# Layer 0's SwiGLU channel mixer in seven half-size products, beside plain context columns, with the layer norms around it in stages

## The chip, the core and the metric

The kernel runs on one core of one Trainium2 chip. A core has five engines, each with its own in-order queue: TensorE (PE; PEld is its weight load), VectorE (DVE), ScalarE (ACT), GpSimd (POOL) and SyncE (SP), which here only issues DMAs. TensorE writes into 8 PSUM banks of 128 x 512 floats; everything else works from SBUF. The metric is the device time in microseconds of one execution, median over runs. The profile is of one such execution.

## What is computed

A trunk of two layers over 1024 latent tokens and 256 context tokens, width 1024. Layer 0 has a recurrent and gated mixer, layer 1 attention; each layer ends with a SwiGLU channel mixer of hidden width 2816. Context tokens need layer 0 whole, and of layer 1 only keys and values. In layer 0, for the latent tokens (the context has the same with its own gates):

```python
def swiglu(h, w_in, w_out):
    gate, up = jnp.split(h @ w_in, 2, axis=-1)
    return (jax.nn.silu(gate) * up) @ w_out
...
        h = layer_norm(alpha * h + g1 * y, ln1_g[l], ln1_b[l])
        h = layer_norm(alpha * h + g2 * swiglu(modulate(h, sh2, sc2), ffn_w_in[l], ffn_w_out[l]),
                       ln2_g[l], ln2_b[l])
```

## The kernel before

All products are of float32 numbers split in two: a rounded high part (`rnd`: on ACT L69, on DVE L71) and the rest (`rest`, L77, on DVE), both float32r, and each product is three matmuls, `mm3` (L80 high by high, L81 high by low, L82 low by high). Tokens stand in ten blocks of 128: 0 to 3 and 4 to 7 are latent, 8 and 9 are the context.

Layer 0 after its mixer runs so. `layer0_out` does the out-projection (tiles `op`) for blocks 0 to 3, then for 4 to 9; ACT copies the banks out (L897), POOL multiplies by the gate (L699). `ln_steps` is the layer norm, a list of small steps that other loops call one by one (`pump`): on DVE the residual (L726), the statistics (L729) and the normalising (L743), on PE eight transposes for each block (`lnT`, L755), on ACT the modulation (L760) and the rounding into the operand tiles `ah`, on DVE the rests `al`, on POOL the affine part (L781, L782). `ffn` is the channel mixer. It runs twice, for blocks 0 to 3 (512 columns) and for 4 to 9 (512 and 256 columns). For each of 22 hidden tiles of 128 it loads three weight tiles (`fraw`), splits them (`fwh`, `fwl`), makes gate and up (`fi`: 8 slices of the contraction, 3 matmuls each, for either), applies SiLU (L1000) and the product (L1003); for two hidden tiles together it then multiplies into the output (`fo`), whose banks DVE adds to the sums in SBUF (L1035). The layer norm of blocks 4 to 9 runs inside the first of these calls; the second layer norm of blocks 0 to 3 inside the second; that of blocks 4 to 9 inside layer 1's input projection (`layer1_in`, tiles `l`), which does the units of blocks 0 to 3 first.

Layer 1's channel mixer, which the change doesn't touch, is already done by a recursion in the manner of Strassen, for its 1024 latent tokens: the tokens, the contraction and the gate and up columns are each cut in half, and seven products of sums and differences take the place of eight (`fi_jobs`, `fo_jobs`; the stationary tiles are `sop` and `fop`, sums of token halves are `T`). The hidden numbers go through HBM (`sd_d`) between the halves. Its code and its trace (2402 us to the end) stand beside layer 0's.

Of the kernel before, what the change touches and what calls it, by code (L numbers as in the profile page):

```python
# [37 lines left out]
def kernel(  # L38
# [64 lines left out]
    sd_d = dram.tile([NHT // 2, 7, 128, 512], F32, name="sd_d")  # L103
    qt_d = dram.tile([16, 128, LAT], F32, name="qt_d")
# [584 lines left out]

    def gate_rows(l, piece, ws):  # L690
        g = {}
        for w in ws:
            g[w] = lnp.tile([128, D], F32, tag=f"g{w}", name=nm("gate"))
            a = ada_d[2 * l + w:2 * l + w + 1, piece * D:(piece + 1) * D]
            nc.sync.dma_start(out=g[w], in_=a.broadcast_to([128, D]))
        return g

    def gate_mul(a, bb, hs, g):
        nc.gpsimd.tensor_tensor(out=a[:, hs], in0=a[:, hs], in1=g[int(bb >= 8)][:, hs], op=ALU.mult)  # L699

    def ln_steps(l, g, b, blocks, acc, mod, aT, src=None, dst=None, alpha=False, late=False, stats=None):

        C = {}

        def consts():
            C["g"] = lnp.tile([128, D], F32, tag="lng", name=nm("lng"))
            nc.sync.dma_start(out=C["g"], in_=g[l:l + 1, :].broadcast_to([128, D]))  # L710
            C["b"] = lnp.tile([128, D], F32, tag="lnb", name=nm("lnb"))
            nc.sync.dma_start(out=C["b"], in_=b[l:l + 1, :].broadcast_to([128, D]))

        def load(bb):
            h = lnp.tile([128, D], F32, tag="hin", name=nm("hin"))
            nc.sync.dma_start(out=h, in_=h_rows(src, bb))
            C["h", bb] = h

        def s0(bb):
            if src is not None:  # L720
                load(bb)

# [41 lines left out]
        def s5(bb):  # L764
# [5 lines left out]
            if not late:  # L770
                s55(bb)
# [19 lines left out]
        if now:  # L791
            consts()
# [1676 lines left out]
```

## Time and profile before

| | us |
|---|---|
| median of 3 runs | 3067.03 |
| lowest, highest | 3063.13, 3068.0 |
| the profiled execution's own time | 3063.5 |
| its span in the trace | 3061.6 |
| layer 0's channel mixer in the trace (first `fi` to last `fo`) | 694.7 to 1656.4 |

Mean granted clock of TensorE over the span: 0.982 of full speed. Times in the rows count from the span's start. A busy PE means that some matmul was under way; matmuls overlap, so the spacing of their starts, not their duration, is what each costs.

### The profile page before, as it was taken

What the parts mean: (1) busy time and instruction counts of PE and PEld (TensorE: products, weight loads), DVE (VectorE), ACT (ScalarE), POOL (GpSimd) and SP (SyncE); (2) the same over time, 40 slices, a digit from 0 to 9 for tenths busy, and PEclk for the clock granted to TensorE, in tenths of its full rate; (3) what the DMA queues carried; (4) which work ended last, traced back from release to release, by engine and by line L of the source; (5) the groups of instructions that cost most, each with busy time, mean ns of one, the idle gap of its engine ahead of it and who ended that gap; (6) DMA issues with size and microseconds to landing.
All of it is one profiled execution on the core that took longest, in us unless ns stands there. A gap on an engine that the chain in (4) does not pass through costs nothing. (4 is left out here: it accounts for less than half of the span.)

```text
span 3061.6 us, 37592 instructions
## 1 busy us (share of the span) xinstructions
PE 2897.3 (95%) x14341; PEld 2340.7 (76%) x14341; DVE 2100.9 (69%) x2742; ACT 1135.8 (37%) x2027; POOL 779.0 (25%) x757
## 2 busy tenths in 40 slices
PE   7999999987999999999999888898889899999997
PEld 4777777876888878888888777666767688888886
DVE  4898843658555566444446876999994777787778
ACT  2555522443211122111112535777773522222433
POOL 5323223246000022000003463777770000000002
PEclk9999999999999999999999999999999999999999
DMA  6344446753333332222223335021102243454854
GB/s 222 126 139 147 158 139 201 229 166 115 119 109 89 105 102 90 62 63 62 70 83 98 103 124 137 18 54 42 34 25 97 90 118 112 153 181 148 298 174 120
DMA packets 314931, 361.37 MB, mean 118 GB/s; under 512 B 16592, under 2 KB 230440, under 8 KB 309632
## 3 DMA queue, kind: packets, MB, share of 16 engines
q1 hardware_dynamic: 306496, 346.33, 35.9%
q0 software_dynamic: 2880, 5.31, 0.9%
q10 hardware_dynamic: 5376, 7.34, 0.7%
q8 instruction: 113, 1.85, 0.2%
q14 instruction: 66, 0.54, 0.1%
HBM read 295.14 MB, written 63.78 MB: 117 GB/s over the span
## 5 line engine op out<-in xcount | busy, mean ns | idle before, releaser
L80 PE MATMUL fi<-ah,fwh 128*128 128x512 f32 (+1 forms) x1056 | 382.4, 362 | 10.3 <-DVE fwh L71 10.3
L82 PE MATMUL fi<-ah,fwl 128*128 128x512 f32 (+1 forms) x1056 | 382.1, 362 | 6.4 <-DVE fwl L77 6.4
L81 PE MATMUL fi<-al,fwh 128*128 128x512 f32 (+1 forms) x1056 | 381.0, 361 | 0.0
L77 DVE TENSOR_TENSOR fwl<-fraw,fwh 128x1024 fp32r<-128x1024 f32 x132 | 168.6, 1277 | 204.4 <-ACT fwh L69 199.5
L699 POOL TENSOR_TENSOR acc<-acc,gate 128x512 f32<-128x512 f32 x40 | 61.1, 1561 | 876.3 <-DVE acc L1035 780.3
L80 PEld LDWEIGHTS fi<-ah,fwh 128*128 128x128 f32 x1056 | 201.2, 191 | 44.8 <-issue 7.8
L82 PEld LDWEIGHTS fi<-ah,fwl 128*128 128x128 f32 x1056 | 201.0, 190 | 42.0 <-DVE fwl L77 9.3
L81 PEld LDWEIGHTS fi<-al,fwh 128*128 128x128 f32 x1056 | 201.3, 191 | 33.1
L1000 ACT ACTIVATE sil<-fi 128x512 f32<-128x512 f32 x66 | 34.7, 526 | 504.7 <-PE fi L82 502.5
L1035 DVE TENSOR_TENSOR acc<-acc,fo 128x512 f32<-128x512 f32 x200 | 134.1, 685 | 81.5 <-PE fo L82 81.5
L73 POOL TENSOR_SCALAR th<-tf 128x512 fp32r<-128x512 f32 x236 | 165.1, 710 | 97.9 <-ACT tf L1761 93.9
L77 DVE TENSOR_TENSOR tl<-tf,th 128x512 fp32r<-128x512 f32 x204 | 171.2, 853 | 13.4 <-POOL th L73 12.4
L80 PE MATMUL ip<-ah,whi 128*128 128x512 f32 (+1 forms) x480 | 175.2, 365 | 3.6 <-ACT ah L69 3.5
L80 PE MATMUL fo<-fwh,hh 128*128 128x512 f32 x440 | 171.8, 390 | 0.1
L81 PE MATMUL ip<-al,whi 128*128 128x512 f32 (+1 forms) x480 | 171.4, 357 | 0.4 <-DVE al L77 0.4
L82 PE MATMUL fo<-fwh,hl 128*128 128x512 f32 x440 | 171.5, 390 | 0.0
L81 PE MATMUL fo<-fwl,hh 128*128 128x512 f32 x440 | 171.2, 389 | 0.0
L82 PE MATMUL ip<-ah,wlo 128*128 128x512 f32 (+1 forms) x480 | 170.4, 355 | 0.0
L1761 ACT COPY tf<-T 128x512 f32<-128x512 f32 x236 | 133.3, 591 | 41.7 <-PE T L1756 24.8
L80 PE MATMUL fi<-ah,sop 128*128 128x512 f32 x352 | 138.3, 393 | 4.8 <-ACT sop L69 4.8
L2291 POOL DMA_DIRECT2D acc<-h_d x16 | 14.2, 905 | 502.8 <-DMA wt<-sd_d 453.8
L1756 PE MATMUL T<-ident,P 128*128 128x128 f32 x944 | 140.5, 275 | 1.1 <-ACT tf L1761 0.4
(388 smaller groups left out, 7738.2 us busy)
## 6 DMA issues: line engine op xcount, KB each, us to landing
fraw<-in_ffn_w_in_dram SPq DMA_DIRECT2D x88, 512.0 KB
adaraw<-in_ada_w_dram SPq DMA_DIRECT2D x40, 1024.0 KB
fraw<-in_ffn_w_out_dram SPq DMA_DIRECT2D x44, 512.0 KB
sraw<-in_ffn_w_in_dram SPq DMA_DIRECT2D x44, 512.0 KB
wt<-sd_d SPq DMA_DIRECT2D x77, 256.0 KB
wt<-in_ffn_w_out_dram SPq DMA_DIRECT2D x55, 256.0 KB
h_d<-acc SPq DMA_DIRECT2D x26, 512.0 KB
sd_d<-hp SPq DMA_DIRECT2D x22, 512.0 KB
```

The source lines that it names most:

```text
L73: nc.gpsimd.tensor_scalar(out=o, in0=i, scalar1=1.0, scalar2=0.0, op0=ALU.mult, op1=ALU.add)
L77: e.tensor_tensor(out=o, in0=i, in1=hi.bitcast(F32), op=ALU.subtract)
L80: nc.tensor.matmul(ps, lhsT=sh, rhs=mh, start=start, stop=False)
L81: nc.tensor.matmul(ps, lhsT=sh, rhs=ml, start=False, stop=False)
L82: nc.tensor.matmul(ps, lhsT=sl, rhs=mh, start=False, stop=stop_)
L699: nc.gpsimd.tensor_tensor(out=a[:, hs], in0=a[:, hs], in1=g[int(bb >= 8)][:, hs], op=ALU.mult)
L1000: nc.scalar.activation(out=sil[si][:, :n], in_=ps_[:, :n], func=AF.Silu)
L1035: nc.vector.tensor_tensor(out=acc[bb][:, ns], in0=acc[bb][:, ns], in1=ps_, op=ALU.add)
L1756: nc.tensor.transpose(ps_[:, x_ * 128:(x_ + 1) * 128], st["P", i, h][:, j * 128:(j + 1) * 128], ident)
L1761: nc.scalar.copy(out=tf, in_=st.pop(("T", i, j)))
L2291: nc.gpsimd.dma_start(out=acc[bb][:, hs], in_=h_rows(3, bb)[:, hs], accum_op=ALU.add)
```

## The change

Layer 0 gets the seven products too. For the 1024 latent tokens the input half takes seven products of 4 slices of the contraction for each hidden tile in place of two times eight slices on both token halves; the 256 context columns are multiplied as before, by the four quarters A11, A12, A21, A22 of the weights (`context`). The hidden numbers, 512 latent and 128 context columns wide, go out to HBM (`sd0_d`) and come back in 77 steps of the output half, each of 15 matmuls into five banks, with a 512-wide weight tile and a 640-wide operand tile loaded and split for each step; here the context is folded into the seven products, one block in each half. The gate products now take the PSUM bank on DVE, the residual is added by an accumulating DMA that POOL issues (`add_rows`), the normalising moves from DVE to ACT, and the affine part moves from POOL to DVE. The layer norms run in stages: `tick` moves each block one stage on, twice in each job. `layer1_in` starts with blocks 4 to 7. In the diff, lines of code that only allocate are left out.

```diff
+    def add_rows(acc, stage, bb, h_):
+        hs = half_cols(h_)
+        nc.gpsimd.dma_start(out=acc[:, hs], in_=h_rows(stage, bb)[:, hs], accum_op=ALU.add)
...
+        groups = [TOK1, CTXB + TOK2]
+        LASTK = 3
+        seq = [(gi, nh, k) for gi in range(2) for nh in range(2) for k in range(12)][2:]
...
+        def u4a(bb):
+            o = blk_tg(bb)[1]
+            c = slice(o, o + 128)
+            (yh, yl), (b11, b11l) = aT[1], (t.bitcast(F32)[:, 0:4, c] for t in aT[0])
+            a, b = C["a", bb, 0], C["a", bb, 1]
+            t1, t2 = (ln0.tile([128, 4, 128], F32, tag=t, name=nm(t)) for t in ("t1", "t2"))
+            C["t", bb] = t1, t2
+            sub(t1, a, b11)
+            sub(t1, t1, b11l)
+            rnd("a", yh[:, 0:4, c], t1)
+            rnd("a", yh[:, 4:8, c], b)
+            sub(t2, b, t1)
+            rnd("a", T["T2"][0][:, :, c], t2)
+            sub(a, b, a)
+            rnd("a", T["T3"][0][:, :, c], a)
...
+        wait = [lambda bb: None] * 3
+        plain = wait + [s1, s2, s3, lambda bb: high_of(aT, C, bb), lambda bb: low_of(aT, C, bb)]
+        other = wait + [s1, s2, s3, u4a, u4b]
+        came = [0]
+        def tick():
+            one = False
+            for x in sorted(active, key=lambda x: (x[1] > 3, x[2])):
+                st_ = other if 4 <= x[0] < 8 else plain
+                if st_[x[1]] is s3:
+                    if one:
+                        continue
+                    one = True
+                st_[x[1]](x[0])
+                x[1] += 1
+                if x[1] == len(st_):
+                    active.remove(x)
...
+            mul(acc[bb][:, hs], ps_, gates[int(bb >= 8)][:, hs])
+            add_rows(acc[bb], 0, bb, nh)
+            if nh:
+                came[0] += 1
+                active.append([bb, 0, came[0]])
...
+            if gi and nh and k >= 12 - LASTK:
+                if k == 11:
+                    aT[1], aT[2] = new_aT(1), new_aT(2)
+                    for j, bb in enumerate(blocks):
+                        for i_ in range(i - LASTK + 1, i + 1):
+                            step_mm(j, i_)
+                        evac(bb, nh, bks[j], gates)
+                        tick()
...
+        def make_t4(bb):
+            c = slice(blk_tg(bb)[1], blk_tg(bb)[1] + 128)
+            t = P["fi"].tile([128, 4, 128], F32, tag=("old", "s4")[bb % 2], name=nm("t4"))
+            b21h, b21l = (x.bitcast(F32)[:, 4:8, c] for x in aT[0])
+            t2h, t2l = (x.bitcast(F32)[:, :, c] for x in T["T2"])
+            sub(t, b21h, t2h)
+            add(t, t, b21l)
+            sub(t, t, t2l)
+            split(B["T4"][0][:, :, c], B["T4"][1][:, :, c], t)
...
+        def done(what, j):
+            a, b = tA[j], tB[j]
+            if what == 2:
+                if j == 0:
+                    gates_in()
+                at(2, fn(gated, b, 0))
+                at(7, fn(statistics, FO["p"], acc2[b], C2, b, 0))
+            if what == 3:
+                at(1, fn(gated, b, 1))
+                for d, f in ((3, f1), (4, f2), (5, f3), (6, f4), (7, f5)):
+                    at(d + 2 * j, fn(f, b))
+            if what == 0:
+                at(1, fn(gated, a, 0))
+                at(5, fn(statistics, FO["p"], acc2[a], C2, a, 0))
+            if what == 1:
+                if j == 0:
+                    for k in sorted(plan):
+                        for f in plan.pop(k):
+                            f()
+                gated(a, 1)
...
+        def second(h):
+            for i, n in enumerate(("A21", "A22")):
+                t = P["zh"].tile([128, 2, 512], F32R, tag=("zA", "zB")[i], name=nm("sop"))
+                split(t[:, 0, :], t[:, 1, :], raws[h, 1][:, i * 512:i * 512 + 512])
+                opnd[h, n] = (t[:, 0, :], t[:, 1, :])
+            g, u = raws[h, 0], raws[h, 1]
+            sub(u[:, :512], g[:, :512], u[:, :512])
+            sub(u[:, 512:], u[:, 512:], u[:, :512])
+            add(g[:, :512], u[:, 512:], g[:, :512])
+            sub(g[:, 512:], g[:, 512:], u[:, 512:])
...
+        FACT = {1: ("A11", "B11"), 2: ("A12", "B21"), 5: ("S1", "T1"), 3: ("S4", "B22"), 6: ("S2", "T2"), 7: ("S3", "T3"),
+                4: ("A22", "T4")}
+        def context(h):
+            ps_ = bank("fi")
+            bh, bl = B["ctx"]
+            for i, n in enumerate(("A11", "A12", "A21", "A22")):
+                hi, lo = opnd[h, n]
+                if i == 2:
+                    tick()
+                for k in range(4):
+                    c = slice(k * 128, (k + 1) * 128)
+                    kk = 4 * (i % 2) + k
+                    mm3(ps_[:, 256 * (i // 2):256 * (i // 2) + 256], hi[:, c], lo[:, c], bh[:, kk, :], bl[:, kk, :],
+                        kk == 0, kk == KD - 1)
+            yield
+            hp = P["zh"].tile([128, 2, 640], F32, tag="hp", name=nm("hp"))
+            tmp["hp", h] = hp
+            v = lambda t: t.rearrange("p (a n) -> p a n", a=2)
+            nc.scalar.activation(out=hp[:, :, 512:640], in_=v(ps_[:, 0:256]), func=AF.Silu)
+            mul(hp[:, :, 512:640], hp[:, :, 512:640], v(ps_[:, 256:512]))
...
+        REST = ("c", 5, 3, 6, 7, 4)
+        seq = [(h, p) for h in range(E) for p in (1, 2)]
+        for h in range(NHT):
+            seq += [(h, p) for p in (REST if h < E else (1, 2) + REST)]
+        where = {x: j for j, x in enumerate(seq)}
+        ahead = [[] for _ in seq]
+        def put(at_, f):
+            ahead[at_].append((0, f))
+        for h in range(NHT):
+            a0 = where[h, 1]
+            if h >= E:
+                put(a0 - 9, fn(raw, h, 0))
+                put(a0 - 9, fn(raw, h, 1))
+            put(max(a0 - (3 if h >= E else 2), 0), fn(pair, h, 1 if h else 0, ("A11", "A12"), 0))
+            z = where[h - 1, 4] + 1 if h else 2
+            put(z, fn(second, h))
+            put(z, fn(pair, h, 2, ("S1", "S4"), 0))
+            put(where[h, 6] - (3 if h else 2), fn(pair, h, 0, ("S3", "S2"), 1))
+            if h >= NP:
+                put(where[h, 6], fn(old, h))
...
+        order = [0, 1, 5, 3, 4, 2, 6]
+        prods = (1, 7, 6, 4, 5, 2, 3)
+        wsrc = {1: (0, 0), 7: (1, 1), 6: (0, 0), 4: (1, 0), 5: (1, 1), 2: (1, 0), 3: (1, 1)}
+        LAST = 4
+        NS = 7 * NP
...
+        def load(s_):
+            x, i = divmod(s_, NP)
+            t = X[s_] = slot(s_)
+            load_w(t[:, 0:512], i, *wsrc[prods[x]])
+            nc.sync.dma_start(out=t[:, 512:1152], in_=sd0_d[i, order[x]])
...
+                for j in range(5):
+                    if x and i == 0 and j >= 2:
+                        evac(x - 1, j - 2)
+                    mms(s_, j)
+                if x and i == 1:
+                    evac(x - 1, 3)
+                    evac(x - 1, 4)
+                tick(s_)
...
+            ahead.append((6, fn(load, s_)))
+            if prods[s_ // NP] in (7, 6, 4, 5):
+                ahead.append((4, fn(comb, s_)))
+            ahead += [(3, fn(high, s_)), (2, fn(low, s_))]
...
-    in_units = [("k", 0), ("cq", 0), ("dq", 0), ("dq", 1), ("k", 2), ("k", 1), ("cq", 1), ("v", 2), ("v", 0), ("v", 1)]
+    in_units = [("k", 1), ("cq", 1), ("dq", 1), ("dq", 0), ("k", 2), ("k", 0), ("cq", 0), ("v", 2), ("v", 1), ("v", 0)]
...
-        aT0 = layer0_out(bks)
-        pairs = [[2 * i, 2 * i + 1] for i in range(NHT // 2)]
...
-        ffn(0, [(h, [(0, 0, 512)]) for h in pairs], aT0, accA, before=load_gates, ended=to_gate(accA))
...
-        ffn(0, [(h, [(1, 0, 512), (2, 0, 256)]) for h in pairs], aT0, accB, before=load_first, ended=ended)
...
+        aT1, acc, ready, pieces, fo, tq, affine_consts, K, close_fo = layer0_rest(bks)
```

On ACT, where the out-projection ends and the channel mixer starts, before: `acc` are the sums of the out-projection, `sil` and `hh` the hidden numbers of the first tile, `a` and `ah` the layer norm of blocks 4 to 9.

```order
L897 COPY acc_756_4970<-op_5019 128x512
L1000 ACT_TABLE_LOAD
L1000 ACTIVATE sil_5445<-fi_5420 128x512
L69 CAST hh_5493<-sil_5445 128x512
L1000 ACTIVATE sil_5539<-fi_5514 128x512
L69 CAST hh_5585<-sil_5539 128x512
L760 ACTIVATE a_877_5594<-lnT_5589,modc 128x128 x4
L69 CAST ah_827_5388<-a_877_5594 128x4x128
L760 ACTIVATE a_879_5605<-lnT_5600,modc 128x128 x4
L69 CAST ah_827_5388<-a_879_5605 128x4x128
```

After, at the same place, from the second block's normalising (L720) on: `sop` are the weights' first splits, `p` the first product's copy, `a`, `ah` and `acc` the layer norm of blocks 8, 9, 4 and on.

```order
L720 ACTIVATE acc_763_5018<-acc_763_5018,nb_5443,rs_5399 128x1024
L69 CAST sop_5474<-sraw_5466 128x1024
L69 CAST sop_5477<-sraw_5470 128x1024
L69 CAST ah_837_5333<-a_847_5427 128x4x128
L69 CAST ah_837_5333<-a_849_5437 128x4x128
L734 ACTIVATE a_866_5500<-lnT_5495,modc 128x128 x4
L734 ACTIVATE a_868_5510<-lnT_5505,modc 128x128 x4
L720 ACTIVATE acc_764_5021<-acc_764_5021,nb_5516,rs_5419 128x1024
L1511 COPY p_870_5525<-fi_5480 128x512
L69 CAST ah_837_5333<-a_866_5500 128x4x128
L69 CAST ah_837_5333<-a_868_5510 128x4x128
L734 ACTIVATE a_874_5542<-lnT_5537,modc 128x128 x4
```

Before, the layer norm of blocks 4 to 9 stood among the hidden tiles' work and nothing in the first `ffn` call read its result. After, its 6 blocks stand in one run, and the weights' splits and the copies of the first products stand among them.

On DVE, within one hidden tile (of blocks 4 to 9 before): `fraw` are loaded weights, `sil` the gate, `hl` the low part of the hidden numbers.

```order
L77 TENSOR_TENSOR fwl_9991<-fraw_9766,fwh_9990 128x1024
L77 TENSOR_TENSOR fwl_10051<-fraw_9826,fwh_10050 128x1024
L71 CAST fwh_10056<-fraw_9892 128x1024
L77 TENSOR_TENSOR fwl_10057<-fraw_9892,fwh_10056 128x1024
L1003 TENSOR_TENSOR sil_10021<-sil_10021,fi_10062 128x512
L77 TENSOR_TENSOR hl_10089<-sil_10021,hh_10088 128x512
L1003 TENSOR_TENSOR sil_10048<-sil_10048,fi_10092 128x256
L77 TENSOR_TENSOR hl_10119<-sil_10048,hh_10118 128x256
```

After, from the last product of one hidden tile into the next: `hp` are the tile's hidden numbers, `sraw` the loaded weights, `sop` their splits, `old` and `s` what is stored for the output half.

```order
L1128 TENSOR_TENSOR hp_7897<-p_1141_7827,fi_7981 128x512
L1131 TENSOR_TENSOR hp_7897<-hp_7897,sil_7842 128x512
L77 TENSOR_TENSOR sop_7997<-sraw_7781,sop_7997 128x512
L77 TENSOR_TENSOR sop_8000<-sraw_7781,sop_8000 128x512
L1125 TENSOR_TENSOR sraw_7781<-sraw_7779,sraw_7781 128x512
L1125 TENSOR_TENSOR sraw_7781<-sraw_7781 128x512
L1128 TENSOR_TENSOR sraw_7779<-sraw_7781,sraw_7779 128x512
L1125 TENSOR_TENSOR sraw_7779<-sraw_7779,sraw_7781 128x512
L77 TENSOR_TENSOR sop_8007<-sraw_7779,sop_8007 128x1024
L1125 TENSOR_TENSOR old_7938<-hp_7897,old_7938 128x640
L1128 TENSOR_TENSOR old_7938<-old_7938 128x640
L1125 TENSOR_TENSOR s_1165_8025<-hp_7897,old_7938 128x640
```

The sums and differences of weight halves and of hidden numbers are new on DVE, ahead of the split that the next products need.

## Rows read from the trace of the kernel before

**Rows 1.** The page, part 1: busy time, share of the span, instructions.
```profile
PE 2897.3 (95%) x14341; PEld 2340.7 (76%) x14341; DVE 2100.9 (69%) x2742; ACT 1135.8 (37%) x2027; POOL 779.0 (25%) x757
```

**Rows 2.** Windows of 50 us in steady channel-mixer stages, layer 0 first.
```profile
core 0: us, PE busy (x) PEld busy (x) DVE busy (x) ACT busy (x) POOL busy (x), PEclk, DMA share, GB/s
800.00:850.00 50.00, 50.00 (x217) 40.52 (x216) 25.78 (x32) 7.08 (x10) 0.00 (x0) 1.00 0.36 105
...
2500.00:2550.00 50.00, 50.00 (x222) 41.42 (x221) 39.48 (x53) 13.61 (x18) 4.21 (x2) 1.00 0.36 108
```

**Rows 3.** Groups by line and shape, TensorE: count, busy us, mean ns, idle before.
```profile
L80 PE MATMUL fi<-ah,fwh 128*128 128x512 f32 x704 | 283.7, 403 | 10.3 <-DVE fwh L71 10.3
L80 PE MATMUL fo<-fwh,hh 128*128 128x512 f32 x440 | 171.8, 390 | 0.1
```

**Rows 4.** Timeline of TensorE in layer 0: start, duration, engine, line.
```profile
814.50 0.39 PE L80 MATMUL fo<-fwh,hh 128*128 128x512 f32 x1
...
817.90 0.39 PE L80 MATMUL fo<-fwh,hh 128*128 128x512 f32 x1
...
1381.22 0.40 PE L80 MATMUL fi<-ah,fwh 128*128 128x512 f32 x1
...
1386.84 0.28 PE L80 MATMUL fi<-ah,fwh 128*128 128x256 f32 x1
...
1389.66 0.39 PE L80 MATMUL fo<-fwh,hh 128*128 128x512 f32 x1
```

**Rows 5.** Timeline of TensorE in layer 1's input half.
```profile
2600.18 0.39 PE L80 MATMUL fi<-ah,sop 128*128 128x512 f32 x1
...
2603.58 0.39 PE L80 MATMUL fi<-ah,sop 128*128 128x512 f32 x1
```

**Rows 6.** Windows of 50 us at the start of layer 0's channel mixer.
```profile
650.00:700.00 50.00, 41.64 (x164) 32.68 (x163) 24.54 (x24) 19.59 (x33) 15.51 (x9) 0.90 0.53 172
700.00:750.00 50.00, 44.73 (x192) 35.13 (x190) 43.06 (x48) 19.37 (x43) 25.79 (x16) 0.93 0.43 127
750.00:800.00 50.00, 41.91 (x174) 32.98 (x175) 36.97 (x38) 15.82 (x35) 18.64 (x9) 0.90 0.40 127
```

**Rows 7.** Timeline of ScalarE: one block of layer 1's layer norm, then splits.
```profile
2392.97 0.62 ACT L69 CAST ah<-a 128x512 fp32r<-128x512 f32 x1
2393.49 0.61 ACT L69 CAST T<-t 128x512 fp32r<-128x512 f32 x1
...
2394.53 1.24 ACT L2024 ACTIVATE acc<-acc,nb,rs 128x1024 f32<-128x1024 f32 x1
2396.69 2.90 ACT L2041 ACTIVATE a<-lnT,modc 128x128 f32<-128x128 f32 x8 [0.92 <-PE lnT L2033]
...
2403.02 1.04 ACT L69 CAST sop<-sraw 128x1024 fp32r<-128x1024 f32 x1 [0.76 <-DMA sraw<-in_ffn_w_in_dram]
...
2416.59 1.28 ACT L1146 ACT_TABLE_LOAD   x1
```

**Rows 8.** Issues of DMA: operation, count, size, median us to landing.
```profile
acc<-h_d POOLq DMA_DIRECT2D x16, 256.0 KB, 4.7
```

**Rows 9.** Window at the start of layer 1's input half.
```profile
2400.00:2450.00 50.00, 43.02 (x174) 34.18 (x175) 39.17 (x57) 24.90 (x39) 0.00 (x0) 0.90 0.29 80
```

**Rows 10.** Groups by line and shape, VectorE.
```profile
L77 DVE TENSOR_TENSOR sop<-sraw,sop 128x1024 fp32r<-128x1024 f32 x66 | 80.6, 1221 | 15.8 <-ACT sop L69 15.8
...
L77 DVE TENSOR_TENSOR sop<-sraw,sop 128x512 fp32r<-128x512 f32 x22 | 15.9, 723 | 2.6 <-ACT sop L69 2.6
...
L1072 DVE TENSOR_TENSOR sil<-p,fi 128x512 f32<-128x512 f32 x22 | 15.1, 687 | 26.6 <-PE fi L82 26.5
```

**Rows 11.** Window at the start of layer 1's output half.
```profile
2850.00:2900.00 50.00, 50.00 (x222) 41.44 (x221) 39.35 (x45) 25.03 (x26) 0.00 (x0) 1.00 0.83 293
```

**Rows 12.** Windows: second layer norm of blocks 0 to 3; layer 1's input projection.
```profile
1050.00:1200.00 150.00, 144.44 (x718) 120.36 (x717) 97.69 (x108) 36.13 (x75) 40.60 (x24) 0.98 0.32 102
1656.40:1880.00 223.60, 195.43 (x1126) 170.29 (x1124) 156.06 (x203) 97.18 (x195) 109.61 (x85) 0.93 0.46 138
```

More of the change, by code (lines that the diff above doesn't have):

```diff
@@ new lines, in layer0_rest @@
+                        evac(bb, nh, bks[j], gates)
+                tick()
+            if (nh == 1) and k < 2 * len(blocks) and k % 2 == 1 and k // 2 < len(blocks):
+                statistics(ln0, acc[blocks[k // 2]], C, blocks[k // 2], 0)
+            if i in (2, 6, 10):
+                fins.append(mod_cols(*mods.pop(0)))
+            if i in (6, 10, 14):
+                fins.pop(0)()
+        closed("s3", "accA")
+        P["tp"] = opened("tp", "right")
+        for n in ("T2", "T3"):
+            T[n] = [P["tp"].tile([128, 4, 512], F32R, tag=n + x, name=nm(n)) for x in "hl"]
@@ new lines, in layer0_rest, with open_fo, gates_in @@
+        jobs, flush = fi0_jobs(0, B, P, left, lambda: None if "fi" in P else tick(), make_t4, aside)
+        n = (half_cols(0), half_cols(1))
+        tA, tB = [0, 1, 2, 3, 8], [4, 5, 6, 7, 9]
+        FO, K = {}, {}
+        def open_fo():
+            flush()
+            flush()
+            closed("fi", "raw", "stash", "ring")
+            FO["p"] = opened("acc0")
+        def gates_in():
+            K["gate"] = [FO["p"].tile([128, D], F32, tag=f"g{w}", name=nm("gate")) for w in range(2)]
+            gate_rows(K["gate"], 0, 5)
@@ new lines, in layer0_rest, with at, tick2, gated @@
+        late_jobs, acc2, pieces = fo0_jobs(0, P, FO, open_fo, lambda *a: done(*a), lambda s_: tick2(s_), tA, tB)
+        C2, aT1 = {}, {}
+        plan, now = {}, [0]
+        def at(d, *fs):
+            plan.setdefault(now[0] + d, []).extend(fs)
+        def tick2(step):
+            now[0] = step
+            for f in plan.pop(step, ()):
+                f()
+        def gated(bb, h_):
+            a = acc2[bb]
+            mul(a[:, n[h_]], a[:, n[h_]], K["gate"][int(bb >= 8)][:, n[h_]])
+            add_rows(a, 1, bb, h_)
@@ new lines, in layer0_rest, with mk, f, affine_consts @@
+        run_jobs(jobs + late_jobs)
+        closed("tp", "zh")
+        stages = (f1, f2, f3, f4, f5)
+        ready = []
+        def mk(i):
+            def f():
+                for j in range(len(stages) - 1, -1, -1):
+                    if 0 <= i - j < 5:
+                        stages[j](tA[i - j])
+                if i == 5 + len(stages) - 2:
+                    ready.append(True)
+            return f
+        bg.extend([mk(i) for i in range(5 + len(stages) - 1)])
+        def affine_consts():
+            for w, a in ((0, ln2_g), (1, ln2_b)):
+                K[w] = FO["p"].tile([128, D], F32, tag=f"g{w}", name=nm("ln"))
+                nc.sync.dma_start(out=K[w], in_=a[0:1, :].broadcast_to([128, D]))
+                nc.gpsimd.tensor_scalar(out=K[w], in0=K[w], scalar1=ALPHA, scalar2=None, op0=ALU.mult)
```

820 lines of the change are left out of this document (461 added, 359 removed).

## The prediction

> **What bounds the kernel now.** I read the page's busy times first: TensorE is busy 95% of the span and no other engine 70% [rows 1]. Then windows inside the two channel mixers. There PE is busy 50.00 of 50 us at the full granted clock, in layer 0 and in layer 1's seven-product form alike, and DVE has 39.48 of 50 us in the latter [rows 2]. So both stages go at the pace of the matmuls, and the form that layer 0 is to get has already run here without a PE gap. Then the spacing of matmul starts, since busy time counts overlaps: layer 0's 704 first-line input matmuls are put down with 403 ns each [rows 3], but 24 of them take 1381.22 to 1386.84, 0.2342 us each; 24 of 256 columns take 0.1175 each; the output half's take 3.40 us for 15, 0.2267 [rows 4], and layer 1's input products also 0.2267 [rows 5]. Last, the places where PE isn't full: the start of layer 0's mixer, with 8.4, 5.3 and 8.1 us of 50 idle and the clock at 0.90, 0.93, 0.90 [rows 6], and layer 1's input projection [rows 12].
>
> **What the change removes.** *Input half.* Before, each hidden tile takes 2 token halves x 2 (gate, up) x 8 slices x 3 = 96 matmuls of 512 columns; after, 7 x 4 x 3 = 84. Over 22 tiles that is 2112 (three lines of the 704 in [rows 3]) against 1848. The new ones have layer 1's form and operands of the same kind, so I give them its spacing [rows 5]: 2112 x 0.2342 = 494.6 becomes 1848 x 0.2267 = 418.9, **-75.7 us**. The nearest other row is the old spacing [rows 4]; with it the term is -61.8. The context's 1056 matmuls of 256 columns stay, at 0.1175.
>
> *Output half.* 22 x 10 blocks x 2 column halves x 3 = 1320 (three lines of 440 [rows 3]) becomes 77 steps x 15 = 1155: 165 x 0.2267 = **-37.4 us** [rows 4].
>
> Here the Trainium skill has a rule that speaks against the size. TensorE: Matmul & The Clock Gate, section Back-to-back issue gap, gives about 131 ns as the sustained spacing of 512-column matmuls between weight loads. By it the 429 dropped matmuls would be worth 56 us and the whole sum would come to about 3000. No stretch in the rows runs below 226 ns, so the measured spacing decides.
>
> **What it adds in the steady loops, and what hides it.** *Input half.* DVE per hidden tile: three rests of 1024 (1.22), two of 512 (0.72), some thirteen sums and products of 512 (0.69), one of 256 for the context (estimate 0.4) and up to three of 640 (estimate 0.86): 3.7 + 1.4 + 9.0 + 0.4 + 2.6 = 17.1 us, with the spare residual work 18.4 [rows 10]. PE needs 84 x 0.2267 + 48 x 0.1175 = 24.7 us. The tightest chain starts at the end of product 4: two sums, two rests, four weight sums, ACT's cast (1.04 [rows 7]) and its rest make 7.8 us until S1 is there; products 1, 2 and the context cover 2 x 2.72 + 5.64 = 11.1. So it costs nothing; were the cover gone, each us of lateness would cost 22.
> *Output half.* Each step has 15 x 0.2267 = 3.40 us of PE. DVE has two rests and sometimes a weight sum, 1.6 to 2.3 us, and bank sums, gates and statistics (some 80 operations over 262 us), 0.7 a step. DMA brings 262 + 328 kB a step, 173 GB/s, and 250 GB/s in the first eleven steps, which fill another weight tile. Layer 1's mixer ran at 293 GB/s with PE at 50.00 of 50 [rows 11]. Nothing again; the price without cover is a rival below.
>
> **The out-projection's end.** This is what I think the change pays for. Before, the layer norm of blocks 4 to 9 lies under an `ffn` call that doesn't need it; idle plus low clock (mean 0.91: some 27 us at the lower of its two levels, worth up to 13) made 22 to 35 us [rows 6]. After, the products with T1 need all of blocks 4 to 7, and only four products and one context product stand ahead. I count ACT's queue: normalising 1.24, eight modulations 2.90 and casts that start 0.52 apart [rows 7], so 5.2 us for blocks 8 and 9 and 6.2 for each of four others, 35; the weights' casts 4.2, a table load 1.28, copies and SiLUs 2.4, and 0.9 of waiting for transposes in each block: 48 us. It starts about 12 us after the last group's matmuls: the statistics of block 8 stand in DVE's queue behind the fourth block's gate product, at 4 x 9 x 0.2267 + 0.7 = 8.9 us; the residual's DMA (4.7 us to land [rows 8]) is there by 8.3. So T1 is whole near 58 us. PE's own work until then is 12.2 + 10.9 + 5.6 and 48 transposes (estimate 6): 35. It waits some 22 us. Then T4, made on DVE late (four blocks of 2.8 us beside 6 us of other work, under 10.9 us of products): 5 us; the second hidden tile's weights 2; and a clock as low as at layer 1's start (0.90 of 50 us, 5 us [rows 9]). Sum 34, bounds 25 and 50. Against 22 to 35 before I take **0**, with -10 and +15.
>
> **The other joints.** The second layer norm of blocks 0 to 3 leaves the `ffn` loop, where 5.6 us were idle and 3 lost to the clock [rows 12]: -8. Its successor, blocks 4 to 7 and 9 within the last output steps, loads ACT with 5.2 us for two steps, beside 2.4 us of casts, under 6.8 us of matmuls and 1 of transposes: just covered, 2 us. The way from input to output half waits for the last hidden numbers: 3. Together **-3**. Layer 1's projection lost 28.2 us idle and up to 16 to the clock [rows 12]; after, its first two weight pieces are split ahead and its first units' blocks are ready, five blocks of layer norm are left in place of six, and their affine work on DVE takes the place of what DVE drops. I take **-8**; bounds -25 and +15.
>
> **Sum**, against the profiled execution's 3063.5: 3063.5 - 75.7 - 37.4 + 0 - 3 - 8 = 2939.4. The median of the runs is 3.5 above that execution, so **2943 us**.
>
> **Rivals.**
> *A dearer joint.* ACT's chain is the longest thing here that nothing covers. If it takes 50 us of loss, or the new products keep 0.2342, the time is 2957 to 2975. For it: PE gets bursts of six matmuls between transposes, each behind a normalising on ACT. Against: layer 1's same joint idled only 7 us in its 50 [rows 9], with two blocks more but 5 us of matmuls between blocks.
> *A cheaper one.* Both projections' ends give back more: 2905 to 2920.
> *The loops aren't covered.* S1 or a bank sum late by 2 to 4 us in each hidden tile: +44 to +88, 2987 to 3031. Against it stands 3.3 us of slack in the worked chain.
> *Slower: the output half is fed too slowly.* Its 77 steps load 48.3 MB. At 108 GB/s, as in [rows 2], they take 447 us in place of 262: 3128. It decides below 125 GB/s. Against it, 293 GB/s [rows 11].
> *No gain.* Lateness that happens to eat the 124 us: within 0.2%, about what a measurement of this kernel can tell from no change.
> *The skill's spacing* (131 ns): 3000; no row bears it out.
>
> **How the numbers follow.** My forecast, 2920 to 2960: 0.53. Dearer joint, 2955 to 2980: 0.24. Cheaper: 0.08. Loops uncovered: 0.08. Slower: 0.04. No gain: 0.02. The skill's spacing: 0.01. The range 2915 to 2990 holds the first two, half the cheaper case and a little of the uncovered loops, about 0.82. Faster 0.94, same 0.02, slower 0.04.
>
> **What would show it.** Starts of `fi` matmuls 0.2267 apart, PE 50.00 of 50 through both halves, 1848 + 1056 and 1155 matmuls. Between the last `op` and the first T1 product, PE waiting for ACT's normalising and casts at each block's transposes, 20 to 25 us in sum. Wrong would be: waits for `sop` or `fow` inside the loops, `al` or stream tiles awaited from DMA, or layer 1's projection longer than 224 us.

## The result, and the profile after

The changed kernel takes 2980.34 us (median of 4 runs, 2979.26 to 2986.51) against 3066.03 for the kernel before on the same chip: ratio 0.9725, 95% interval 0.9709 to 0.9742. The range of the prediction holds it, the forecast of 2943 does not: 86 us came where 124 had been worked out. The profiled execution's span fell from 3061.6 to 2978.5 us, 83.1 us, and the stages can be compared by the first and last matmul of each in the timeline of TensorE. The table has them for every kernel of this study (us, between starts read to 0.1 us, each from one profiled execution; the channel mixer is layer 0's, from the first `fi` to the first `l`, which is layer 1's input projection).

| kernel | `op` stage | last `op` to first `fi` | channel mixer | `l` stage | median of runs |
|---|---|---|---|---|---|
| before | 185.0 | 2.0 | 962.0 | 205.0 | 3066.0 |
| after | 199.8 | 10.3 | 862.2 | 195.7 | 2980.3 |
| e1 four raw tiles | 186.8 | 9.3 | 864.4 | 194.6 | 2974.2 |
| e2 layer norm later | 196.9 | 11.1 | 863.0 | 196.5 | 2979.1 |
| e3 loads ahead of a store | 200.8 | 7.0 | 863.2 | 194.9 | 2980.0 |
| e4 the three together | 183.2 | 7.0 | 862.4 | 195.8 | 2963.0 |
| e5 and normalising on VectorE | 181.0 | 5.3 | 858.5 | 196.4 | 2956.3 |
| e6 e4 and T4 early | 183.5 | 7.0 | 861.2 | 196.9 | 2962.3 |
| e7 two matmuls of three | 199.5 | 10.3 | 709.5 | 197.7 | 2835.4 |
| e8 weights 32 bytes lower | 200.2 | 11.1 | 871.3 | 195.5 | 2992.7 |
| e9 e5 and sums later | 181.2 | 5.2 | 858.6 | 196.1 | 2953.8 |
| e10 e9 and lows on GpSimd | 180.0 | 5.3 | 859.8 | 196.7 | 2953.0 |
| e11 before, two row buffers | 195.7 | 2.1 | 958.7 | 203.9 | 3076.1 |

So the mixer gave 99.8 us and the `l` stage 9.3, and the out-projection with its end took 23.1 back. The page's busy times, to be held against [rows 1]:

```profile
PE 2793.1 (94%) x13912; PEld 2260.6 (76%) x13912; DVE 2138.9 (72%) x2995; ACT 1281.4 (43%) x2229; POOL 663.0 (22%) x729
```

Groups by line and shape on TensorE, the counterpart of [rows 3]. The first two hold layer 1's 352 and 264 too, so that layer 0 has 352 + 264 triples of matmuls, 1848, and the output half 3 x 385 = 1155, as worked out:

```profile
L80 PE MATMUL fi<-ah,sop 128*128 128x512 f32 x704 | 279.7, 397 | 16.3 <-ACT sop L69 13.3 <-ACT ah L69 3.1
...
L80 PE MATMUL fi<-T,sop 128*128 128x512 f32 x528 | 206.6, 391 | 8.8 <-ACT T L69 7.2 <-ACT sop L69 1.6
...
L80 PE MATMUL fo<-fow,fos 128*128 128x512 f32 x385 | 150.6, 391 | 3.5 <-DVE acc L1128 2.2 <-ACT fos L69 1.3
```

Windows of 50 us in layer 0's steady loops (columns as in [rows 2]): two in the input half, one at the start of the output half. TensorE has no gap at 139 GB/s nor at 331, and VectorE works 31.5 to 35.2 of 50 us:

```profile
850.00:900.00 50.00, 50.00 (x267) 43.37 (x266) 31.51 (x44) 13.92 (x22) 0.00 (x0) 1.00 0.32 92
...
1250.00:1300.00 50.00, 50.00 (x267) 43.33 (x267) 34.78 (x49) 13.75 (x21) 0.00 (x0) 1.00 0.43 139
1300.00:1350.00 50.00, 50.00 (x222) 41.40 (x221) 35.24 (x51) 23.17 (x39) 0.00 (x0) 1.00 0.92 331
```

The timeline of TensorE there: twelve starts of a product take 1100.45 to 1103.17, fifteen of an output step 1400.33 to 1403.73, both 0.2267 us each. The context's starts of 256 columns lie 0.120 apart (1089.82 to 1094.86 for 42; the mean over the input half is 0.1198):

```profile
1089.82 0.28 PE L82 MATMUL fi<-ah,sop 128*128 128x256 f32 x1
...
1094.86 0.28 PE L82 MATMUL fi<-ah,sop 128*128 128x256 f32 x1
...
1100.45 0.39 PE L80 MATMUL fi<-T,sop 128*128 128x512 f32 x1
...
1103.17 0.39 PE L80 MATMUL fi<-T,sop 128*128 128x512 f32 x1
...
1400.33 0.39 PE L80 MATMUL fo<-fow,fos 128*128 128x512 f32 x1
...
1403.73 0.39 PE L80 MATMUL fo<-fow,fos 128*128 128x512 f32 x1
```

Where time was lost, in windows of 25 us of the changed kernel: first the out-projection (first group, then the start of the second at 600), then the start of the mixer.

```profile
550.00:575.00 25.00, 21.80 (x89) 16.46 (x90) 14.13 (x34) 8.13 (x14) 3.67 (x4) 1.00 0.75 190
...
600.00:625.00 25.00, 15.01 (x64) 11.79 (x65) 8.29 (x18) 20.53 (x44) 3.16 (x8) 0.80 0.53 183
...
700.00:725.00 25.00, 16.17 (x64) 12.31 (x62) 10.81 (x22) 10.57 (x21) 7.58 (x13) 0.80 0.89 189
725.00:750.00 25.00, 12.85 (x56) 10.38 (x56) 14.86 (x28) 22.12 (x45) 2.04 (x4) 0.83 0.21 85
750.00:775.00 25.00, 21.68 (x102) 18.03 (x101) 21.32 (x34) 11.61 (x23) 0.00 (x0) 0.83 0.14 42
775.00:800.00 25.00, 16.55 (x83) 13.36 (x82) 17.99 (x26) 5.62 (x8) 0.00 (x0) 0.86 0.00 1
```

In the kernel before, the out-projection had no gap from 550 to 625:

```profile
550.00:575.00 25.00, 25.00 (x111) 20.42 (x110) 14.17 (x33) 10.19 (x18) 1.30 (x1) 1.00 0.66 201
...
600.00:625.00 25.00, 25.00 (x120) 20.89 (x119) 16.22 (x23) 13.61 (x29) 7.58 (x6) 1.00 0.53 175
```

What TensorE waited for (us in total, times, longest) in the changed kernel, from 500 to 640 and then from 640 to 800:

```profile
PE lnT L729 <- ACT acc L720: 6.5, 1, 6.5
PE lnT L729 <- ACT a L734: 5.5, 5, 2.3
PE op L80 <- ACT wh L69: 4.9, 2, 2.8
```

```profile
PE lnT L729 <- ACT acc L720: 13.0, 5, 4.0
PE fi L80 <- ACT sop L69: 8.6, 2, 7.9
PE fi L80 <- ACT T L69: 7.2, 1, 7.2
PE fi L80 <- ACT ah L69: 3.1, 1, 3.1
```

Behind ScalarE stand other things. In the first group it waits for the rows of the mixed tokens, by its waits from 515 to 600; the same line of the kernel before has 9.5 us in 3 times:

```profile
ACT mh L69 <- DMA mraw<-mix_d: 32.8, 14, 5.6
```

The change explains that: the ring of `mraw`, the tiles that these rows are loaded into, went from three tiles to two. It is one of the allocations that the diff above leaves out, and the prediction passed it over. At the start of the mixer, SP holds the first weight loads (L1442) behind the store of block 8 (L833), which waits until that block's residual has landed and it has been normalised. SP's queue in the timeline, idle from 691.7 to 708.9:

```profile
691.28 0.43 SPq L798 DMA_DIRECT2D wraw<-in_ev_w_out_dram  x1
708.93 0.32 SPq L833 DMA_DIRECT2D h_d<-acc  x1
709.35 7.81 SPq L1442 DMA_DIRECT2D sraw<-in_ffn_w_in_dram  x4
```

ScalarE's timeline behind the last `op` shows both kinds of idle time in its chain, for loads (3.18, 2.84) and for VectorE (3.49, 5.03):

```profile
707.66 1.24 ACT L720 ACTIVATE acc<-acc,nb,rs 128x1024 f32<-128x1024 f32 x1 [11.97 <-DVE nb L719]
...
716.86 1.04 ACT L69 CAST sop<-sraw 128x1024 fp32r<-128x1024 f32 x1 [3.18 <-DMA sraw<-in_ffn_w_in_dram]
720.74 1.04 ACT L69 CAST sop<-sraw 128x1024 fp32r<-128x1024 f32 x1 [2.84 <-DMA sraw<-in_ffn_w_in_dram]
...
750.64 1.04 ACT L69 CAST sop<-sraw 128x1024 fp32r<-128x1024 f32 x1 [3.49 <-DVE sraw L1125]
756.71 0.62 ACT L69 CAST ah<-t 128x512 fp32r<-128x512 f32 x1 [5.03 <-DVE t L1125]
```

### The profile page after: what moved, and what is told of

Same layout as the page of the kernel before. It is cut to its first block, busy times and chain, and to the rows that moved or that the text cites. A ratio compares the mean times of both kernels' runs of the same rounds, so it can differ in the third digit from the quotient of the medians.

```text
span 2978.5 us, 37852 instructions
## 1 busy us (share of the span) xinstructions
PE 2793.1 (94%) x13912; PEld 2260.6 (76%) x13912; DVE 2138.9 (72%) x2995; ACT 1281.4 (43%) x2229; POOL 663.0 (22%) x729
## 5 line engine op out<-in xcount | busy, mean ns | idle before, releaser
L80 PE MATMUL fi<-ah,sop 128*128 128x512 f32 (+1 forms) x1056 | 379.2, 359 | 16.3 <-ACT sop L69 13.3
L82 PE MATMUL fi<-ah,sop 128*128 128x512 f32 (+1 forms) x1056 | 377.6, 358 | 0.6 <-DVE sop L77 0.5
L81 PE MATMUL fi<-al,sop 128*128 128x512 f32 (+1 forms) x1056 | 377.8, 358 | 0.3 <-DVE al L77 0.3
L69 ACT CAST sop<-sraw 128x1024 fp32r<-128x1024 f32 (+1 forms) x198 | 176.5, 901 | 264.9 <-DVE sraw L1125 195.1
L77 DVE TENSOR_TENSOR sop<-sraw,sop 128x1024 fp32r<-128x1024 f32 (+1 forms) x198 | 203.8, 1047 | 93.6 <-ACT sop L69 93.6
L80 PEld LDWEIGHTS fi<-ah,sop 128*128 128x128 f32 x1056 | 202.7, 192 | 45.5 <-ACT sop L69 14.1
L82 PEld LDWEIGHTS fi<-ah,sop 128*128 128x128 f32 x1056 | 201.8, 191 | 30.9 <-DVE sop L77 2.6
L81 PEld LDWEIGHTS fi<-al,sop 128*128 128x128 f32 x1056 | 202.3, 192 | 28.7 <-DVE al L77 0.8
L80 PE MATMUL fi<-T,sop 128*128 128x512 f32 x528 | 206.6, 391 | 8.8 <-ACT T L69 7.2
L82 PE MATMUL fi<-T,sop 128*128 128x512 f32 x528 | 206.2, 391 | 0.5 <-DVE sop L77 0.5
L81 PE MATMUL fi<-T,sop 128*128 128x512 f32 x528 | 206.4, 391 | 0.0
L77 DVE TENSOR_TENSOR tl<-tf,th 128x512 fp32r<-128x512 f32 x204 | 171.9, 857 | 13.1 <-POOL th L73 12.4
L80 PE MATMUL fo<-fow,fos 128*128 128x512 f32 x385 | 150.6, 391 | 3.5 <-DVE acc L1128 2.2
L82 PE MATMUL fo<-fow,fos 128*128 128x512 f32 x385 | 150.0, 390 | 0.1
L81 PE MATMUL fo<-fow,fos 128*128 128x512 f32 x385 | 149.9, 389 | 0.0
L2119 DVE TENSOR_REDUCE mx<-S 128x1 f32<-128x1024 f32 (+2 forms) x128 | 127.8, 999 | 14.2 <-PE S L2113 13.0
```

The lines of the kernel that those rows point to most:

```text
L69: nc.scalar.copy(out=o, in_=i)
L77: e.tensor_tensor(out=o, in0=i, in1=hi.bitcast(F32), op=ALU.subtract)
L80: nc.tensor.matmul(ps, lhsT=sh, rhs=mh, start=start, stop=False)
L81: nc.tensor.matmul(ps, lhsT=sh, rhs=ml, start=False, stop=False)
L82: nc.tensor.matmul(ps, lhsT=sl, rhs=mh, start=False, stop=stop_)
L2119: nc.vector.tensor_reduce(out=st["mx", i][:, c, h:h + 1], in_=st["sc", i, h][c], axis=AX.X, op=ALU.min)
```

## The experiments

All ratios are to the kernel before, on the same chip as the run. The first four take the out-projection and the start of the mixer apart.

**e1, four raw tiles.** 
```
-            elif i < 4:
-                m, w = (accB.tile([128, 512], F32, tag=f"acc{4 + x_ + 2 * (i // 3)}", ...) ...
...
+            elif gi == 0:
+                t = accB.tile([128, 1024], F32, tag=f"acc{4 + i % 4}", name=nm("mw"))
+                m, w = t[:, 0:512], t[:, 512:1024]
```


> The first group's steps of the out-projection load into four whole accumulator tiles that are still unused, in place of two row buffers and three weight buffers. Theory A (the out-projection is late because SP waits for one of only two row buffers): ScalarE's waits for mraw between 515 and 600 fall from 33 us to under 10, TensorE's three windows from 525 to 600 go from 21.5 to about 24.5 of 25 busy, and the time falls by 7 to 10 us, to 2970 to 2974. Rival (ScalarE's chain at the start of the channel mixer holds everything back, and the out-projection's idle time is made up there): within 2 us of 2980.

Measured: 2974.21, ratio 0.9693 (0.9675 to 0.971). The `op` stage is 13.0 us shorter, 186.8. ScalarE's waits for rows between 515 and 600 fell to two lines (the new tiles are named `mw`):

```profile
ACT mh L69 <- DMA mw<-mix_d: 11.2, 4, 5.5
...
ACT mh L69 <- DMA mraw<-mix_d: 2.1, 1, 2.1
```

The place is as theory A has it: TensorE is busy 24.9 and 25.0 of 25 us from 525 to 575, though only 19.4 in the third window, where the layer norm now starts. Of the time, the median shows 6 us where 7 to 10 were expected, and the trace 13; its execution is the fastest of the four (2965.99 to 2975.15).

**e11, the same cause put into the kernel before.**
```
-                    m = p.tile([128, 768], F32, tag="mraw", bufs=3, name=nm("mraw"))
+                    m = p.tile([128, 768], F32, tag="mraw", bufs=2, name=nm("mraw"))
```


> The kernel before, with two row buffers in the out-projection in place of three, and nothing else changed. If the number of row buffers made the out-projection's first group wait for loads in the changed kernel: the same loss appears here, ScalarE waits 25 to 35 us for mraw in place of 9.5, the stage from the first to the last op matmul grows from 185 to some 193 to 197, and the time rises by 6 to 12 us, to 3072 to 3078. If the other edits there (gates, tick, sources of the first loads) made it: within 3 us of 3066.

Measured: 3076.14 against 3067.26, ratio 1.0032 (1.002 to 1.0043), and the `op` stage 10.7 us longer. ScalarE's waits for rows, 515 to 600:

```profile
ACT mh L69 <- DMA mraw<-mix_d: 27.9, 12, 5.7
```

One buffer fewer, with nothing else changed, makes the waits and 9 to 11 us. With e1 this is shown from both sides.

**e2, the first layer norm later.**
```
-                active.append([bb, 0, came[0]])
+                active.append([bb, -2 * came[0] if bb < 4 else 0, came[0]])
```
(and in `tick` a block whose count is still negative does nothing)


> The first layer norm of blocks 0 to 3 starts two to eight ticks later and one block after the other, in place of four together. Theory B (the four normalisations stand ahead of the next weights' casts on ScalarE, behind residual DMAs that have not landed): TensorE's wait of 6.5 us for normalising near 600 and most of the 5.5 us for modulation go, 600 to 625 is busy 23 or more of 25 at full clock, and the time falls by 8 to 12 us, to 2968 to 2972. Rival (the four blocks' work on ScalarE is too much wherever it stands): the waits move to later steps and the time stays within 3 us of 2980.

Measured: 2979.05, ratio 0.9717 (0.9699 to 0.9736), the `op` stage 2.9 us shorter. The waits for modulation are gone, but those for normalising, from 500 to 640, grew:

```profile
PE lnT L729 <- ACT acc L720: 9.3, 3, 6.9
```

So theory B missed: a later start moves the wait to another step. Beside e1's loads (e4) it shortens the stage from 186.8 to 183.2.

**e3, weight loads ahead of block 8's store.**
```
             turned(ln0, acc[bb], C, bb, 1, 4)
-            nc.sync.dma_start(out=h_rows(1, bb), in_=acc[bb])
+            if bb < 4 or not held:
+                nc.sync.dma_start(out=h_rows(1, bb), in_=acc[bb])
+            else:
+                held.append(bb)
...
         jobs, flush = fi0_jobs(0, B, P, left, lambda: None if "fi" in P else tick(), make_t4, aside)
+        for bb in held[1:]:
+            nc.sync.dma_start(out=h_rows(1, bb), in_=acc[bb])
+        held.clear()
```


> SP issues the store of block 8 after the first four weight loads of the channel mixer, in place of ahead of them. Theory C (the loads stand behind a store that waits for block 8's normalising): the first loads start near 692 and have landed by 707, ScalarE's first weight cast waits for nothing, the first seven-product matmul starts 3 to 5 us earlier, and the time falls by 3 to 6 us, to 2974 to 2977. Rival (ScalarE's queue of normalising, modulation and casts sets the pace): the first product starts earlier, but the later blocks' transposes come no sooner, and the time stays within 2 us of 2980.

Measured: 2980.03, ratio 0.9719 (0.9703 to 0.9735). The first `fi` comes 7.0 in place of 10.3 us after the last `op`, yet TensorE's waits at 640 to 800 stay elsewhere:

```profile
PE lnT L729 <- ACT acc L720: 13.1, 5, 4.1
PE fi L80 <- ACT T L69: 7.4, 1, 7.4
PE fi L80 <- ACT sop L69: 5.3, 2, 4.6
```

The loads do stand behind the store, and it costs next to nothing: from the last `op` to the first `l` only 2.3 us went. The rival, ScalarE's queue, stands.

**e4, the three together.**

> The three edits together. If the three losses are separate and each theory holds: the sum of the three gains, 18 to 28 us, so 2952 to 2962. If the rival holds at the start of the channel mixer (ScalarE's chain): only the first two count, 2960 to 2967. If none holds: 2978 to 2982.

Measured: 2963.04, ratio 0.9662 (0.9647 to 0.9677): 17 us, just short of the first case and within the second, which also has the place right: 16.6 us of it lie in the `op` stage.

**e5, ScalarE's chain made shorter** (e4's edits, and):
```
         def s2(bb):
-            normalise(ln0, acc[bb], C, bb)
+            nc.vector.tensor_scalar(out=acc[bb], in0=acc[bb], scalar1=C.pop(("mv", bb))[:, 0:1],
+                                    scalar2=C.pop(("rs", bb)), op0=ALU.subtract, op1=ALU.mult)
```


> The kernel with the three edits together, and the normalising of layer 0's first layer norm moved from ScalarE to VectorE, which has 10 of 25 us free there. Theory R (ScalarE's chain of normalising, modulation and casts sets the start of the channel mixer): each of five blocks gives ScalarE 1.24 us back, TensorE's wait of 13 us for normalising falls to 6 or less, and the time falls by 4 to 7 us from 2963, to 2956 to 2959. Theory C (loads and weights set it): within 2 us of 2963. Worse than 2965 would say that VectorE's own queue takes ScalarE's place.

Measured: 2956.25, ratio 0.9642 (0.9628 to 0.9657), 7 us less; 5.6 of them lie between the last `op` and the first `l` (869.4 to 863.8). TensorE's waits, 680 to 800:

```profile
PE fi L80 <- ACT T L69: 7.3, 1, 7.3
PE fi L80 <- ACT ah L69: 6.4, 1, 6.4
PE fi L80 <- ACT sop L69: 4.2, 2, 3.5
```

The 13 us for normalising have gone, and part came back as a wait for the last casts. It came out as theory R has it: 6.2 us taken off ScalarE there brought 5.6. But the edit also takes the step `nb` and a hand-over from VectorE to ScalarE out of each block's chain, so this run does not tell ScalarE's load from the length of the chain. VectorE needs 0.76 us where ScalarE took 1.24 [rows 7]:

```profile
689.26 0.76 DVE L831 TENSOR_SCALAR acc<-acc,mv,rs 128x1024 f32<-128x1024 f32 x1
```

**e6, T4 early** (e4's edits, and):
```
-            put(where[0, 3] + (i + 1) // 2, fn(make_t4, b))
+            put(where[0, 3], fn(make_t4, b))
```


> The kernel with the three edits together, and the four blocks of T4 all made ahead of product 3 of the first hidden tile, in place of one ahead of 3, two ahead of 6 and one ahead of 7. If T4 is late because of its place in VectorE's queue (each block stands behind the sums of a product that TensorE has yet to finish): TensorE's wait of 7 us for T falls to under 3, and the time falls by 3 to 6 us, to 2957 to 2960. If it is late because VectorE has too much work there: the wait moves to the products before, within 2 us of 2963.

Measured: 2962.26, ratio 0.9663 (0.9649 to 0.9678): no gain. The wait for T fell from 7.1 to 5.5 us only, so its place in the queue is not the main cause:

```profile
PE fi L80 <- ACT T L69: 5.5, 1, 5.5
```

**e9, the first weight sums later** (e5's edits, and):
```
-            put(z, fn(second, h))
-            put(z, fn(pair, h, 2, ("S1", "S4"), 0))
+            put(z, fn(second, h))
+            z = z if h else where[0, "c"]
+            put(z, fn(sums, h))
+            put(z, fn(pair, h, 2, ("S1", "S4"), 0))
```
where `sums` holds the last four lines of `second`.

> As the run with normalising on VectorE, and the four weight sums of the first hidden tile with the split of S1 and S4 put behind the layer norm of blocks 6 and 7 in the program, just ahead of the context product, in place of between blocks 5 and 6. If these sums, which stand in VectorE's queue ahead of block 6's differences while ScalarE waits 3.5 and 5.0 us for VectorE, make blocks 6 and 7 late: their casts come 4 to 8 us earlier, TensorE's wait of 6.4 us for ah falls below 3, and the time falls by 3 to 5 us, to 2951 to 2954. If all of VectorE's work has to be done before T1 and T4 whatever its order: within 2 us of 2956.

Measured: 2953.76, ratio 0.963 (0.9617 to 0.9643), 2.5 us less in the median, with intervals of the ratio that overlap, and none between the last `op` and the first `l` (863.8 both times), where the gain was expected. The wait for `ah` has become one for the weights that were put behind, beside 6.2 us for T:

```profile
PE fi L80 <- ACT sop L69: 12.8, 3, 8.6
```

**e10, low halves on GpSimd** (e9's edits, and `rest("p", ...)` for T2 and T3).

> The same, and the low halves of T2 and T3 in the first layer norm (8 operations) computed on GpSimd, which is idle there, at 1.3 us each in place of 0.6 on VectorE. If VectorE's sum of work is what T1 and T4 wait for: it is 5 us less, TensorE's wait of 7 us for T falls to 3 to 4, and the time is 2 to 4 us below the run without it. If GpSimd's access slows VectorE, or T2 is late from GpSimd: same or slower by up to 4 us.

Measured: 2953.02, ratio 0.9632 (0.9619 to 0.9645): the same as e9. The wait for T is as long, 6.2 us, and one for T at the transposes grew:

```profile
PE lnT L729 <- ACT T L69: 7.4, 2, 4.4
```

Which of VectorE's steps sets the last 6 us of T stays open; e9 and e10, which cannot be told apart, are the fastest versions of the study that make every product.

The last two concern the terms that held.

**e7, how much cover the loops have.**
```
-                mm3(out, hi[:, c], lo[:, c], bh[:, k, :], bl[:, k, :], k == 0, k == 3)
+                nc.tensor.matmul(out, lhsT=hi[:, c], rhs=bh[:, k, :], start=k == 0, stop=False)
+                nc.tensor.matmul(out, lhsT=lo[:, c], rhs=bh[:, k, :], start=False, stop=k == 3)
```
(and the same in the output half's `mms`)

> The changed kernel without the third matmul of each triple in layer 0's seven-product channel mixer (low half of the tokens' numbers in the input half, low half of the weights in the output half); the context's products keep three. Everything else is made as before, so the work of the other engines stays and its cover is a third shorter. If the loops are bound by TensorE with the slack that the prediction gives them (VectorE 15.6 to 17.0 us of what would be 18.3 for a hidden tile; in the output half 2.3 us of 2.27 for a step, so about even): the input half loses 616 x 0.2267 = 140 us, the output half 45 to 80 of its 87, 2760 to 2795. If VectorE or DMA stands close behind TensorE in both: under 100 us in sum, above 2880.

Measured: 2835.35, ratio 0.925 (0.9234 to 0.9265), 145 us less, between the two cases. In the profiled execution, which is 5 us below the median, the output half fell by 54 us (272.8 to 218.4), as expected, the input half by 98 (588.9 to 490.7) of 140. A window and the waits of TensorE from 800 to 1150:

```profile
950.00:1000.00 50.00, 47.39 (x262) 40.02 (x261) 38.00 (x53) 17.85 (x27) 0.00 (x0) 1.00 0.39 111
```

```profile
PE fi L1471 <- DVE sop L77: 14.0, 26, 0.8
```

A hidden tile has 104 matmuls then, and windows with 262 in 50 us give 19.8 us for it (20.1 for each of the later tiles): 1.4 more than TensorE's 18.4, in many small waits for split weights. So the changed kernel's 24.8 us have 4.7 to 4.9 of slack over this chain. Some 11 of the missing 42 us lie in the first three hidden tiles, where waits set the pace: they took 109.4 us in place of 117.6, 8.2 less where 3 x 6.35 = 19 us of matmuls had gone.

**e8, where the weights lie.**
```
+        pad = opened("pad", "right").tile([128, 8], F32, name=nm("pad"))
+        nc.vector.memset(pad, 0.0)
         for n in ("ring", "stash", "raw"):
             P[n] = opened(n, "right")
```


> The changed kernel with the ring of split weights of the input half placed 32 bytes lower in each partition, so that in 1584 of its 1848 matmuls of 512 columns the weights' address and that of the moving numbers differ by 32 modulo 64, as all of them did in the kernel before (and in the kernel after none). If that is what made 0.2342 of 0.2267 us: starts lie 0.234 apart in these, 0.2267 in the product of T4, and the time rises by 12 us, to 2992. If the shape of the products makes the pace: 0.2267 throughout, 2978 to 2982.

Measured: 2992.73, ratio 0.9762 (0.9747 to 0.9776), 12.4 us more in the median; the profiled execution has 8.0 more in the input half. In the timeline the twelve starts of a shifted product take 2.80 us, 0.2333 each, and the later starts of T4's product, which is not shifted, are 0.68 apart for three:

```profile
1107.26 0.39 PE L80 MATMUL fi<-T,sop 128*128 128x512 f32 x1
...
1110.06 0.39 PE L80 MATMUL fi<-T,sop 128*128 128x512 f32 x1
...
1114.25 0.39 PE L80 MATMUL fi<-T,sop 128*128 128x512 f32 x1
...
1114.93 0.39 PE L80 MATMUL fi<-T,sop 128*128 128x512 f32 x1
...
1121.22 0.28 PE L80 MATMUL fi<-ah,sop 128*128 128x256 f32 x1
...
1124.02 0.28 PE L80 MATMUL fi<-ah,sop 128*128 128x256 f32 x1
...
1124.62 0.28 PE L82 MATMUL fi<-ah,sop 128*128 128x256 f32 x1
```

So the new spacing came with the new addresses, not with the form of the products. The context's product shows the other side of it: its first 24 matmuls use shifted weights and take 0.1167 us each (1121.22 to 1124.02), its last 24 use weights that did not move and lie 0.120 apart (1124.02 to 1124.62 for five), as all do in the changed kernel. The 256 columns got faster by the shift that made 512 columns slower. By these spacings the shift costs some 9 us (1584 x 0.0066, less 528 x 0.0033); the rest of the 12.4 is not explained.

## Why the prediction was right, and where it was off

**The matmul terms: right, the spacing partly by luck.** The input half's -75.7 and the output half's -37.4 rest on 1848 and 1155 matmuls at 0.2267; both counts and the spacing are in the rows above. The context's 1056, which were to stay at 0.1175, take 0.1198 each, 2.4 us more. By the spacings, the mixer's matmuls took 917.9 us before and take 807.2 now. The reason given ("layer 1's form and operands of the same kind") was not the reason: e8 shows that it is how the two operands lie, and that the changed kernel lays them as layer 1 does was not looked at. The Trainium skill's rule (TensorE: Matmul & The Clock Gate, section Back-to-back issue gap: about 131 ns) would have made the 429 dropped matmuls worth 56 us; the trace does not agree, with 0.2267 us in the steady rows.

**The steady loops: right.** VectorE has 15.6 to 17.2 us in a hidden tile of 24.8 (31.5 to 34.8 of 50), where 17.1 to 18.4 were worked out. The slack of 3.3 us was at least 4.7 (e7). The rivals of uncovered loops and of an output half fed too slowly fall with the windows at 50.00 of 50, at 331 GB/s too.

**The out-projection's end, "I take 0": this step failed.** Its stage and what follows cost 36.5 us more than before, where +15 was the upper bound: 14.8 in the `op` stage, 8.3 between the last `op` and the first `fi`, and 13.4 from there to 830, counted as the time beyond the matmuls at their steady spacing (29.9 before, 43.3 after).
- The `op` stage itself was taken as unchanged, although the diff takes a row buffer away from its first group and puts that group's four layer norms together, ahead of the next casts. The first is 11 to 13 us by stage times (e1, e11), the layer norm 3 to 4 beside it (e4 against e1).
- At the joint I had 34 us of loss after and 22 to 35 before. Summed over the starts from 690 to 830, as time beyond 0.2267, 0.1175 and (transposes) 0.125 us, the loss is 49 after and 28 before (26 with its own 0.2342 for `fi`): the old side was well priced, the new one came out at its upper bound of 50. By terms: TensorE's waits until the product with T1 cost 27.1 us where 22 was taken, the wait for T4 7.4 (5), the second tile's weights 1.6 (2), and the lower clock with all other slow starts 12.9 (5). The granted clock is 0.88 over these 140 us, which makes 34 us at its lower level; I had taken it from a window with 0.90 of 50 us, 10 us. So the rival of the dearer joint had the mechanism; its 2957 to 2975 was passed because the `op` stage came on top.
- What was mis-sized in the waits is ScalarE's chain. I added 48 us for it, of which 5.4 were waiting for transposes (with a start at 12 that makes 60, where I wrote 58). From 707.7 to 762.7, where the product with T1 starts, ScalarE works 39.8 us and is idle for 15.3: 6.0 for weight loads that I did not place in SP's queue, 8.5 for differences and weight sums in VectorE's, 0.8 for a transpose. So the work was less than I had counted, and the waits more. Taking away one of these waits alone gains little, because the others close up (e3, e6, e9, e10); taking the normalising off ScalarE gains nearly all of its time (e5).

**The other joints, -3: about right.** Of [rows 12] the 8.6 us of blocks 0 to 3 left the loop; the output half takes 272.8 us where its matmuls need 261.8, 11 in place of the 5 given to its start and end, of which the transposes of five blocks are about 5. Counted alike, as time beyond the matmuls with the transposes in it, that is 13.6 us before (1050 to 1200) and 11.2 after: -2.4.

**Layer 1's projection, -8: right.** The `l` stage fell by 9.3, from 205.0 to 195.7.

Everything else adds 2.9 us. In sum: -113.1 + 2.4 + 14.8 + 8.3 + 13.4 - 2.4 - 9.3 + 2.9 = -83.0, where the spans differ by 83.1.

## What to carry to other kernels

Counting dropped matmuls at the measured spacing is safe where windows show TensorE full and the operands lie as they did where it was measured; the error lies in the stages that the diff only touches in passing, so read every changed buffer count and every moved step there, and look for what waits for it. A chain over several engines has to be laid out with the queue of each, SP's too, and with the idle time in it, since the sum of one engine's work is only its lower bound. Where several queues close up behind each other, putting one load or sum earlier moves the wait; taking work off the engine that has the longest chain shortened it here (e5).

## What was not expected of the hardware

The spacing of 512-column matmuls went with the place of the operands. Starts were 0.2267 us apart in layer 0's products of the changed kernel, where the addresses of weights and moving numbers in a partition are equal modulo 64 bytes (as the built programs have them), and 0.2333 and 0.2342 in the input halves of e8 and of the kernel before, where they differ by 32. Matmuls of 256 columns went the other way: 0.1198 with equal addresses, 0.1167 and 0.1175 where they differ by 32. The place was changed by itself in e8 alone; 32 bytes of padding made 12 us in the median, some 9 by the spacings. It is not the whole rule: the `l` stage of the changed kernel has equal addresses and a median spacing of 0.233, which stays open.

And one row buffer of three was worth 9 us (e11), in a stage where ScalarE works 9 to 11 of 25 us and DMA moves 169 to 227 GB/s.
